# Rounding the stick-breaking heads of a decoder layer in pairs and placing their operands by transfers

## The chip, the cores and the metric

The kernel runs on one core of one Trainium2 chip. The core has TensorE (PE; its weight loads are listed apart as PEld), VectorE (DVE), ScalarE (ACT), GpSimd (POOL) and SyncE (SP), which here issues transfers only. The metric is the device time of one execution in microseconds (us). Inputs and outputs are float32.

## The reference

One layer of a decoder with two groups of attention heads, for 512 tokens of width 2048, and a last RMSNorm:

```python
h = rmsnorm(x, ln_mix)
sb_q, sb_k, sb_v, sw_q, sw_k, sw_v = split(h @ w_in)
# group A, 16 heads of 64: causal stick-breaking
z = (q * 64 ** -0.5) @ k.T
log_one_minus = where(s < t, log_sigmoid(-z), 0)
survive = reverse_cumsum(log_one_minus) - log_one_minus
sb_o = where(s < t, exp(log_sigmoid(z) + survive), 0) @ v
# group B, 16 query heads on 4 key heads: window of 128, ALiBi, sinks, softmax
sw_o = softmax(scores - slope * distance, with a sink) @ v
x = x + concat(rmsnorm(sb_o), rmsnorm(sw_o)) @ w_out
x = x + (silu(h2 @ w_gate) * (h2 @ w_up)) @ w_down      # h2 = rmsnorm(x, ln_ffn)
return rmsnorm(x, ln_final)
```

## The kernel before

**Products.** TensorE multiplies in a rounded float32 form. To keep the accuracy, an operand is split into a high part (a rounded copy) and a low part (the operand minus that copy), and a product is three matmuls: high by high, high by low, low by high. Weights stream from HBM in slabs of 128 x 1024 elements into three buffers `raw`; ScalarE writes the high part `whi` (L215) and VectorE the low part `wlo` (L216), both with two buffers.

**The queue of slabs.** All projections stand in one list, `queue`. Each entry is a slab with its eight products. `step()` emits one product. At the third product of slab i it emits the loads of slabs i+1 and i+2 and the rounding (`split`) of slab i+1. `pull(ns)` emits products worth so many nanoseconds, and `drain(mark)` emits all up to a mark. `defer(n, fn)` calls `fn` after n more products. Loads go through `dma()` (L100), which issues from SP and keeps the order of the program on that queue; the instructions of the other engines may be put in another order by the scheduler that lays out the program, within what their data allow.

**The stick-breaking stage** (about 155 to 433 us). `sb_begin(h)` starts head h. The queries and keys of a pair of heads come out of two PSUM banks into a tile `qk` (L683 and L686), head 2u in rows 0 to 63 and head 2u+1 in rows 64 to 127. A score matmul contracts over 128 rows, so for each head three tiles are made: `q1` has the high part of the queries in both halves, `q2` the low part in both halves, and `ks` the high part of the keys in the rows of the head and the low part in the others. `stack_two` (L692 to L695) and `stack_one` (L701, L702) write them by ScalarE and VectorE, 64 rows at a time. Two matmuls (L846, L847) then give the whole score.

Each head has three jobs, key blocks 3 and 2 together, then 1, then 0. A job passes through the score matmuls, a mask (L852), three ScalarE steps, the split of the log terms (L866, L867, L872), the sums (L904), the exponential and its split (L918, L919, L924) and the product with the values (L934). Jobs are interleaved over three turns of one loop, and in each turn three pulls put products of the queue between the parts. `sb_begin` is called three jobs before the first job of its head. The products in between belong to the later pairs' queries and keys (`add_qk`), then to the window group's keys, and then to its values (`add_swv`).

**The window group's values.** `add_swv` uses `add_tok` with `halves=True`: two blocks of 128 tokens share a PSUM bank, and the last slab runs block by block. `done` evacuates a block by L267 and L268 into `swv`.

**The window stage.** It makes a table of distances `dist` (L977 to L981, first read at L1076), stacks keys and queries of the first key group with the same two helpers, and adds the slabs of query groups 2 and 3 to the queue. Its first score matmuls are at L1061 and L1062.

The window stage's filler continues with the output projection; the feed-forward part, from about 700 us on, is written out in a fixed order and is not touched.

Of the kernel before, what the change touches and what calls it, by code (L numbers as in the profile page):

```python
# [8 lines left out]
F32 = mybir.dt.float32  # L9
F32R = mybir.dt.float32r  # L10
BF16 = mybir.dt.bfloat16
I32 = mybir.dt.int32
AF = mybir.ActivationFunctionType
ALU = mybir.AluOpType
AX = mybir.AxisListType

P = 128
# [4 lines left out]
HD = 64  # L22
# [7 lines left out]
FAR = 1.0e32  # L30
# [7 lines left out]
def tile_hymba(ctx: ExitStack, tc: tile.TileContext, x, ln_mix, w_in, sb_norm, swa_norm,  # L38
# [36 lines left out]
    def pz():  # L75
        return zs[1].tile([P, 512], F32, tag="z", name="z", bufs=4)
# [17 lines left out]
    def tmp(dt=F32, name="t"):  # L94
        return phase[1].tile([P, 512], dt, tag="t", name=name, bufs=phase[2])
# [3 lines left out]
    def dma(out, in_):  # L99
        tc.keep_in_program_order(nc.sync.dma_start(out=out, in_=in_))  # L100

    def f(ap):
        return ap.bitcast(F32)

    mm = nc.tensor.matmul
    V = nc.vector
    A = nc.scalar
    G = nc.gpsimd
# [63 lines left out]
    pos = [0, 0]  # L172
# [26 lines left out]
    def split(i):  # L199
        sl = queue[i]  # L200
        if "hi" in sl:
            return
        load(i)
        if sl["prep"] and i:
            sl["prep"]()
        a, b, raw = sl["a"], sl["b"], sl["raw"]
        hi = wp.tile([P, a, b], F32R, tag="whi", name="whi", bufs=2)
        lo = wp.tile([P, a, b], F32R, tag="wlo", name="wlo", bufs=2)
        if i == 0:
            for j in range(a):  # L210
                h_make(j)
                pA.activation(out=hi[:, j, :], in_=raw[:, j, :], func=AF.Copy)
                pV.tensor_tensor(out=lo[:, j, :], in0=raw[:, j, :], in1=f(hi)[:, j, :], op=ALU.subtract)
        else:
            A.activation(out=hi, in_=raw, func=AF.Copy)  # L215
            V.tensor_tensor(out=lo, in0=raw, in1=f(hi), op=ALU.subtract)  # L216
        sl["hi"], sl["lo"] = hi, lo

    def defer(n, fn):
        due.append([n, fn])  # L220
# [39 lines left out]
    def drain(mark=None):  # L260

        mark = len(queue) if mark is None else mark
        while pos[0] < mark:
            step()
# [54 lines left out]
    def h_make(kt):  # L319
        pb = pz()  # L320
        for t in range(NT):
            pT.transpose(out=pb[:, t * P:(t + 1) * P], in_=xs[kt, t], identity=ident)
            warm({(0, 0): 1, (0, 1): 1, (0, 2): 3, (1, 3): 3}.get((kt, t), 0))
        if kt % 4 == 0:
            h8[0], h8[1] = act8("hhi"), act8("hlo")
        h_hi[kt], h_lo[kt] = h8[0][:, kt % 4, :], h8[1][:, kt % 4, :]
        split_scaled(pb, gcol[:, kt:kt + 1], h_hi[kt], h_lo[kt])
        if kt % 4 == 0:
            h8s.append((h8[0], h8[1]))
        left_sums(kt, pb)  # L330
# [33 lines left out]
    def add_tok(src_fn, nslab, a, b, lhs_fn, get_banks, done, prep_fn=None, halves=False, big=False):  # L364

        bk = {}
        t3 = 3 * 0.4215 * b

        def one(t, j, s):
            def go(hi, lo):  # L370
                k = s * a + j
                lh, ll = lhs_fn(k)
                o = bk["b"][t // 2][:, (t % 2) * b:(t % 2) * b + b] if halves else bk["b"][t][:, :b]
                sl = slice(t * P, (t + 1) * P)
                first = k == 0 and not (halves and t % 2)
                mm(o, lhsT=lh[:, sl], rhs=hi[:, j, :], start=first, stop=False, skip_group_check=halves)  # L376
                mm(o, lhsT=lh[:, sl], rhs=lo[:, j, :], start=False, stop=False, skip_group_check=halves)  # L377
                mm(o, lhsT=ll[:, sl], rhs=hi[:, j, :], start=False, stop=(k == nslab * a - 1),  # L378
                   skip_group_check=halves)
                if k == nslab * a - 1:  # L380
                    done(t, o)
                return t3
            return go

        for s in range(nslab):
            if s == nslab - 1 or (s == 0 and queue):
                mms = [one(t, j, s) for t in range(NT) for j in range(a)]
            else:
                mms = [one(t, j, s) for j in range(a) for t in range(NT)]
            pair = ([] if s % 2 == 0 else pair) if big else None  # L390
            queue.append(dict(srcs=[src_fn(s)], a=a, b=b, mms=mms, big=pair,
                              pre=(lambda: bk.update(b=get_banks())) if s == 0 else None, post=None,
                              prep=(lambda s=s: prep_fn(s)) if prep_fn else None))
# [291 lines left out]
    def k_evac(pb, dst):  # L685
        V.tensor_tensor(out=dst, in0=pb, in1=rs1["b"], op=ALU.mult)  # L686

    def stack_two(src, r0, hi, lo):

        s64 = src[r0:r0 + HD]  # L690
        r1 = HD - r0
        A.activation(out=hi[r0:r0 + HD], in_=s64, func=AF.Copy)  # L692
        V.tensor_copy(out=hi[r1:r1 + HD], in_=s64)
        V.tensor_tensor(out=lo[r0:r0 + HD], in0=s64, in1=f(hi)[r0:r0 + HD], op=ALU.subtract)
        V.tensor_copy(out=lo[r1:r1 + HD], in_=f(lo)[r0:r0 + HD])  # L695

    def stack_one(src, r0, st):

        s64 = src[r0:r0 + HD]
        r1 = HD - r0  # L700
        A.activation(out=st[r0:r0 + HD], in_=s64, func=AF.Copy)  # L701
        V.tensor_tensor(out=st[r1:r1 + HD], in0=s64, in1=f(st)[r0:r0 + HD], op=ALU.subtract)  # L702
# [38 lines left out]
    def sbt(dt, name, n=512, bufs=1):  # L741
        return phase[1].tile([P, n], dt, tag=name, name=name, bufs=bufs)
# [62 lines left out]
    kqp = kqs.enter_context(tc.tile_pool(name="kq2", bufs=1, side="right", reuse_waits="tile"))  # L805
# [2 lines left out]
    sb_mark = len(queue)  # L808
    add_swv()
    swv_end = len(queue)  # L810
    pair = [sbt(F32R, name, 512) for name in ("h32", "l32")]
    for t in pair:
        G.memset(f(t)[:, 0:P], 0.0)
    sqA = kqp.tile([P, 512], F32, name="sqA")

    class Head:
        pass

    heads = {}

    def sb_begin(h):
        drain(marks[h // 2])
        H = Head()
        heads[h] = H
        H.r0 = (h % 2) * HD
        qk = qks[h // 2]
        H.q1, H.q2, H.ks = sbt(F32R, "q1", bufs=2), sbt(F32R, "q2", bufs=2), sbt(F32R, "ks", bufs=2)
        stack_two(qk[:, 0, :], H.r0, H.q1, H.q2)
        stack_one(qk[:, 1, :], H.r0, H.ks)
        H.acc = [None] * 3  # L830
        H.blk = [None] * 3

    def span(i):
        return {2: (P, 512), 1: (0, 384), 0: (0, 512)}[i]

    def sb_qk(h, i):
        H = heads[h]
        B = Head()
        H.blk[i] = B
        a, w = span(i)  # L840
        zb = pz()
        B.zb, B.z = zb, zb[:, a:w]
        for k, c0, o in (((3, 256, 0), (2, 256, 256)) if i == 2 else ((i, i * P, 0),)):
            kb = H.ks[:, k * P:(k + 1) * P]
            out = zb[:, o:o + S - c0]
            mm(out, lhsT=kb, rhs=H.q1[:, c0:S], start=(o == 0), stop=False, skip_group_check=True)  # L846
            mm(out, lhsT=kb, rhs=H.q2[:, c0:S], start=False, stop=True, skip_group_check=True)  # L847
# [106 lines left out]
    for j in range(NJ + 2):  # L954
        if j + 3 < NJ and jobs[j + 3][1] == 2:
# [16 lines left out]


    swp = open_phase("swp", 15)
    dist = swp.tile([P, 256], F32, name="dist", bufs=1)
    disti = tmp(I32, "disti")[:, 0:256]
    G.iota(disti, pattern=[[-1, 256]], base=P, channel_multiplier=1)  # L977
    V.tensor_copy(out=dist, in_=disti)
    G.affine_select(out=dist, in_=dist, pattern=[[-1, 256]], compare_op=ALU.is_ge, fill=FAR,
                    base=P, channel_multiplier=1)  # L980
    G.affine_select(out=dist, in_=dist, pattern=[[1, 256]], compare_op=ALU.is_ge, fill=FAR,  # L981
                    base=-1, channel_multiplier=-1)
    sqB = swp.tile([P, 512], F32, name="sqB", bufs=1)
    oB = [swp.tile([P, 4, 512], F32, tag="oB", name="oB", bufs=2) for _ in range(2)]
    kst = [None, None]
# [2 lines left out]
    def stack_keys(c, e):  # L988
        stack_two(kq2[:, c, :], e * HD, kst[c][:, 2 * e, :], kst[c][:, 2 * e + 1, :])
# [7 lines left out]
    def add_swq(g):  # L997
        def done(c, pb):
            if c == 0:
                qst[g] = v8.tile([P, 4, 512], F32R, tag="v8", name="qst")  # L1000
            qf = tmp(name="qf")
            q_evac(pb, qf)
            for e in range(2):
                stack_one(qf, e * HD, qst[g][:, c * 2 + e, :])

        add_feat(win, [(C_SWQ + g * 256, 256)], (lambda: [po(), po()]) if g == 2 else two_m, done)
        smarks[g] = len(queue)

    kst[0], qst[0], qst[1], kst[1] = (v8.tile([P, 4, 512], F32R, tag="v8", name=n) for n in ("kst", "qst", "qst", "kst"))
    stack_keys(0, 0)  # L1010
    stack_queries(0, 0)
    stack_queries(0, 1)
    for g in (2, 3):
        add_swq(g)


    mixA = [None] * 10
# [835 lines left out]
```

## Time and profile before

| | |
|---|---|
| runs | 2003.01, 2003.05, 2002.39 us; median 2003.01 us |
| profiled execution | 2003.03 us, span 2000.9 us |
| TensorE busy | 1983.5 us (99%) |
| VectorE busy | 1479.4 us (74%) |
| ScalarE busy | 1512.2 us (76%) |
| GpSimd busy | 1115.7 us (56%) |

Rows of waits read "engine line <- engine tile line: us in total, times, longest us". A row of the timeline gives the start and the duration in us, engine, line, operation, output and inputs, shape, and in brackets the idle time before it and what ended it. A row of a tile's view gives minimum, median and maximum in ns and the first and last start. A row of stretches gives the stretch, its length, then the busy time of PE, PEld, DVE, ACT and POOL with the number of instructions, the granted clock, the share of the DMA engines and GB/s. Issues of transfers end with KB each and the median us from issue to landing.

### The profile page before, as it was taken

The numbers are of one execution on the slowest core, as the hardware profiler recorded it, in microseconds if no ns is written. First come the engines' busy times: TensorE is split into PE (matmuls) and PEld (weight loads), VectorE is DVE, ScalarE is ACT, GpSimd is POOL, SyncE is SP. The second block draws the span as 40 slices with busy tenths as digits, with TensorE's granted clock in tenths as the row PEclk, the third lists the DMA queues.
The fourth block names the chain that finished last, engine by engine and source line by source line (L and its number), as shares of the span: only waits on it lengthen the run. The fifth ranks groups of instructions, "written<-read, shape, count | busy, mean of one in ns | idle before, by whom it ended". The sixth has DMA issues, their size and how long they took to land.

```text
span 2000.9 us, 29118 instructions
## 1 busy us (share of the span) xinstructions
PE 1983.5 (99%) x10268; PEld 1697.5 (85%) x10268; DVE 1479.4 (74%) x1972; ACT 1512.2 (76%) x2031; POOL 1115.7 (56%) x599
## 2 busy tenths in 40 slices
PE   9999999999999999999999999999999999999998
PEld 8888888888888888888888888888888888888886
DVE  6677787778974787777777777777777867767767
ACT  6766887868762487777777777777777788788787
POOL 2842454520010076575666657566665778878883
PEclk9999999999999999999999999999999999999999
DMA  6412222222334435445354444535444744433423
GB/s 202 146 53 85 64 65 68 70 71 67 106 115 138 143 121 137 128 110 142 100 138 110 127 126 112 141 101 138 109 129 111 271 150 129 167 126 113 177 80 116
DMA packets 283298, 240.22 MB, mean 120 GB/s; under 512 B 11025, under 2 KB 233297, under 8 KB 280721
## 3 DMA queue, kind: packets, MB, share of 16 engines
q1 hardware_dynamic: 281392, 231.52, 38.9%
q0 software_dynamic: 1376, 5.52, 0.9%
q8 instruction: 81, 1.33, 0.3%
q10 hardware_dynamic: 384, 1.34, 0.2%
q14 instruction: 65, 0.52, 0.1%
HBM read 218.40 MB, written 19.92 MB: 119 GB/s over the span
## 4 chain that ended last, share of the span: by engine, by line
PE 93%; DVE 3%; ACT 3%; issue 1%; DVEq 0%; POOL 0%; ACTq 0%; POOLq 0%
PE o L118 36%; PE m L118 30%; PE m L408 3%; PE m L409 3%; PE m L410 2%; PE m L376 2%; PE m L378 2%; PE m L377 2%; PE z L118 1%; PE o L378 1%; PE o L376 1%; PE o L377 1%; PE z L904 1%; PE o L934 1%; PE z L1112 1%
## 5 line engine op out<-in xcount | busy, mean ns | idle before, releaser
L118 POOL TENSOR_TENSOR t<-raw,t 128x1024 f32<-128x1024 f32 x111 | 282.3, 2543 | 281.1 <-ACT hp L118 262.8
L118 DVE TENSOR_TENSOR wlo<-t,hp 128x1024 fp32r<-128x1024 f32 x247 | 301.0, 1219 | 183.2 <-PE o L118 113.6
L118 ACT ACTIVATE whi<-t 128x1024 fp32r<-128x1024 f32 x247 | 261.9, 1060 | 126.3 <-PE o L118 76.3
L118 POOL TENSOR_TENSOR t<-raw,raw 128x1024 f32<-128x1024 f32 x114 | 294.7, 2588 | 23.5 <-issue 12.1
L118 PE MATMUL o<-hca,whi 128*128 128x512 f32 x880 | 307.5, 391 | 0.0
L118 DVE TENSOR_TENSOR wlo<-raw,hp 128x1024 fp32r<-128x1024 f32 x187 | 228.1, 1220 | 91.7 <-issue 52.1
L118 ACT ACTIVATE whi<-raw 128x1024 fp32r<-128x1024 f32 (+1 forms) x189 | 199.8, 1057 | 105.4 <-PE m L118 75.2
L118 ACT ACTIVATE hp<-t 128x1024 fp32r<-128x1024 f32 x247 | 249.1, 1009 | 2.2 <-POOL t L118 2.1
L118 PE MATMUL o<-hca,wlo 128*128 128x256 f32 x880 | 244.0, 280 | 0.0
L118 ACT ACTIVATE hp<-raw 128x1024 fp32r<-128x1024 f32 x191 | 192.9, 1010 | 4.4 <-DMA raw<-in_w_down_dram 3.2
L118 PEld LDWEIGHTS o<-hca,whi 128*128 128x128 f32 x880 | 164.2, 187 | 35.8
L118 PE MATMUL m<-hca,whi 128*128 128x512 f32 x528 | 186.3, 392 | 1.1 <-DVE hca L118 1.1
L118 PEld LDWEIGHTS o<-hca,wlo 128*128 128x128 f32 x880 | 165.6, 189 | 0.4
L215 ACT ACTIVATE whi<-raw 128x1024 fp32r<-128x1024 f32 x87 | 91.7, 1054 | 79.8 <-PE o L378 39.2
L216 DVE TENSOR_TENSOR wlo<-raw,whi 128x1024 fp32r<-128x1024 f32 x87 | 108.7, 1249 | 56.0 <-ACT whi L215 53.7
L118 PE MATMUL m<-whi,dca 128*128 128x512 f32 x592 | 146.9, 389 | 0.0
L118 PE MATMUL o<-whi,dca 128*128 128x512 f32 x592 | 146.9, 389 | 0.0
L118 PE MATMUL m<-hca,wlo 128*128 128x256 f32 x528 | 146.3, 280 | 0.0
L118 PEld LDWEIGHTS m<-whi,dca 128*128 128x128 f32 x592 | 111.1, 188 | 23.1
L118 PEld LDWEIGHTS o<-whi,dca 128*128 128x128 f32 x592 | 111.1, 188 | 23.0
L408 PE MATMUL m<-hhi,whi 128*128 128x512 f32 x320 | 125.9, 393 | 0.7 <-DVE qk L683 0.7
L118 PE MATMUL m<-hcs,whi 128*128 128x512 f32 x352 | 125.9, 392 | 0.0
(371 smaller groups left out, 5225.8 us busy)
## 6 DMA issues: line engine op xcount, KB each, us to landing
raw<-in_w_gate_up_dram SPq DMA_DIRECT2D x348, 256.0 KB, 5.2
raw<-in_w_down_dram SPq DMA_DIRECT2D x68, 512.0 KB, 4.9
raw<-in_w_in_dram SPq DMA_DIRECT2D x35, 512.0 KB, 3.7
raw<-in_w_in_dram SPq DMA_DIRECT2D x66, 256.0 KB, 3.3
raw<-in_w_out_dram SPq DMA_DIRECT2D x32, 512.0 KB, 3.7
aT<-w SPq DMA_DIRECT2D x44, 256.0 KB, 3.4
xd<-aT SPq DMA_DIRECT2D x10, 1024.0 KB, 7.5
rx<-in_w_down_dram SPq DMA_DIRECT2D x20, 512.0 KB, 6.2
```

Of the source, the lines that this page charges most:

```text
L118: return lambda *a, **k: tc.keep_in_program_order(fn(*a, **k))
L215: A.activation(out=hi, in_=raw, func=AF.Copy)
L216: V.tensor_tensor(out=lo, in0=raw, in1=f(hi), op=ALU.subtract)
L376: mm(o, lhsT=lh[:, sl], rhs=hi[:, j, :], start=first, stop=False, skip_group_check=halves)
L377: mm(o, lhsT=lh[:, sl], rhs=lo[:, j, :], start=False, stop=False, skip_group_check=halves)
L378: mm(o, lhsT=ll[:, sl], rhs=hi[:, j, :], start=False, stop=(k == nslab * a - 1), skip_group_check=halves)
L408: mm(o, lhsT=wh, rhs=xh, start=(k == 0), stop=False)
L409: mm(o, lhsT=wh, rhs=xl, start=False, stop=False)
L410: mm(o, lhsT=wl, rhs=xh, start=False, stop=(k == KT - 1))
L904: mm(zb[:, o:o + r.shape[1]], lhsT=lhsT, rhs=r, start=False, stop=last, skip_group_check=True)
L934: mm(H.ob[:, c0:S], lhsT=vb, rhs=r[:, o:o + S - c0], start=(k == 3 and r is B.h), stop=(k == 0 and r is B.l), skip_group_check=True)
L1112: nc.tensor.transpose(out=pb[:, hh * P:(hh + 1) * P], in_=B.s[hh // 2][:, hh % 2, j * P:(j + 1) * P], identity=ident)
```

## The change

Four things are changed.

1. `sb_begin` rounds a pair at once: for an even head, `hi_lo` writes the high parts of the pair's queries and of its keys into a new tile `qkh` (ScalarE, 128 rows each) and leaves the low parts in `qk` itself (VectorE, 128 rows each). A function `place`, called six products later or at the head's first score matmuls at the latest, fills `ks`, `q1` and `q2` by six transfers of 64 rows on SP.
2. In `add_tok` with halves, both blocks of a bank are evacuated after the second one.
3. The table `dist` is made before the stick-breaking loop, in the pool that holds `sqA`, whose tile lends its first half to the integers.
4. At the start of the window stage the slabs of the queries are queued first, and the next slab is rounded before the keys and queries are stacked. That stacking stays with the engines.

```diff
                 if k == nslab * a - 1:
-                    done(t, o)
+                    if not halves:
+                        done(t, o)
+                    elif t % 2:
+                        done(t - 1, bk["b"][t // 2][:, 0:b])
+                        done(t, o)
...
+    def hi_lo(src, hi):
+        A.activation(out=hi, in_=src, func=AF.Copy)
+        V.tensor_tensor(out=src.bitcast(F32R), in0=src, in1=f(hi), op=ALU.subtract)
...
+    dist = kqp.tile([P, 256], F32, name="dist")
+    sqA = kqp.tile([P, 512], F32, name="sqA")
+    disti = sqA[:, 0:256].bitcast(I32)
+    G.iota(disti, pattern=[[-1, 256]], base=P, channel_multiplier=1)
+    V.tensor_copy(out=dist, in_=disti)
+    G.affine_select(out=dist, in_=dist, pattern=[[-1, 256]], compare_op=ALU.is_ge, fill=FAR,
+                    base=P, channel_multiplier=1)
+    G.affine_select(out=dist, in_=dist, pattern=[[1, 256]], compare_op=ALU.is_ge, fill=FAR,
+                    base=-1, channel_multiplier=-1)
...
-        H.q1, H.q2, H.ks = sbt(F32R, "q1", bufs=2), sbt(F32R, "q2", bufs=2), sbt(F32R, "ks", bufs=2)
-        stack_two(qk[:, 0, :], H.r0, H.q1, H.q2)
-        stack_one(qk[:, 1, :], H.r0, H.ks)
+        if h % 2 == 0:
+            qkh[0] = sbt(F32R, "qkh", 1024).rearrange("p (two t) -> p two t", two=2)
+            for c in range(2):
+                hi_lo(qk[:, c, :], qkh[0][:, c, :])
+
+        def place():
+            H.place = None
+            H.q1, H.q2, H.ks = sbt(F32R, "q1", bufs=2), sbt(F32R, "q2", bufs=2), sbt(F32R, "ks", bufs=2)
+            rows = slice(H.r0, H.r0 + HD)
+            for r in (0, HD):
+                dma(out=f(H.ks)[r:r + HD], in_=(f(qkh[0]) if r == H.r0 else qk)[rows, 1, :])
+            for r in (0, HD):
+                dma(out=f(H.q1)[r:r + HD], in_=f(qkh[0])[rows, 0, :])
+            for r in (0, HD):
+                dma(out=f(H.q2)[r:r + HD], in_=qk[rows, 0, :])
+
+        H.place = place
+        defer(6, lambda: H.place and H.place())
...
+        if H.place:
+            H.place()
         zb = pz()
...
     kst[0], qst[0], qst[1], kst[1] = (v8.tile([P, 4, 512], F32R, tag="v8", name=n) for n in ("kst", "qst", "qst", "kst"))
+    for g in (2, 3):
+        add_swq(g)
+    split(pos[0] + 1)
     stack_keys(0, 0)
     stack_queries(0, 0)
     stack_queries(0, 1)
-    for g in (2, 3):
-        add_swq(g)
```

More of the change, by code (lines that the diff above doesn't have):

```diff
@@ L813, in tile_hymba @@
         G.memset(f(t)[:, 0:P], 0.0)
-    sqA = kqp.tile([P, 512], F32, name="sqA")
     class Head:
@@ L819, in tile_hymba @@
     heads = {}
+    qkh = [None]
     def sb_begin(h):
@@ L974, in tile_hymba @@
     swp = open_phase("swp", 15)
[L975 to L982, printed above, removed]
     sqB = swp.tile([P, 512], F32, name="sqB", bufs=1)
```

## The prediction

> **What bounds the kernel now.** I read the page's first section, then the engine's busy time in stretches, then who waits for whom on TensorE alone.
>
> ```profile
> span 2000.9 us, 29118 instructions
> PE 1983.5 (99%) x10268; PEld 1697.5 (85%) x10268; DVE 1479.4 (74%) x1972; ACT 1512.2 (76%) x2031; POOL 1115.7 (56%) x599
> 140.00:160.00 20.00, 20.00 (x91) 16.29 (x91) 15.48 (x23) 11.27 (x19) 0.00 (x0) 1.00 0.30 88
> 240.00:420.00 180.00, 176.63 (x886) 150.34 (x885) 141.81 (x220) 145.99 (x261) 89.62 (x116) 1.00 0.22 65
> 1980.00:2001.00 21.00, 11.52 (x50) 8.94 (x48) 14.06 (x35) 12.79 (x33) 5.55 (x5) 0.90 0.55 200
> PE o L934 <- DVE l L924: 2.6, 4, 1.2
> PE m L376 <- DVE swv L268: 1.6, 1, 1.6
> PE m L408 <- DVE qk L683: 0.7, 2, 0.4
> ```
>
> TensorE (first busy column of a stretch) is idle for 17.4 us of the span, and 9.5 of these are the tail (21.00 minus 11.52), which the change does not touch. No matmul is added or removed. So the change can only win idle time of TensorE in the stick-breaking stage (about 155 to 433 us) and at its end, or add some. There the last three rows are all there is: seven waits, 4.9 us.
>
> The idle column understates a stop, because a matmul's modelled end overlaps the next one's start:
>
> ```profile
> 356.00 0.28 PE L934 MATMUL o<-h,vst 128*128 128x256 f32 x1
> 356.70 0.39 PE L934 MATMUL o<-l,vst 128*128 128x256 f32 x1 [0.43 <-DVE l L924]
> 356.92 0.28 PE L934 MATMUL o<-h,vst 128*128 128x256 f32 x1
> 357.04 0.28 PE L934 MATMUL o<-l,vst 128*128 128x256 f32 x1
> ```
>
> Unhindered, such matmuls start 0.12 us apart (the last two); here 0.70 passed, so 0.58 was lost where the row says 0.43. I add 0.16 for each wait: L934 2.6 + 4 × 0.16 = 3.25, L408 0.7 + 2 × 0.16 = 1.05, L376 1.6 + 0.16 = 1.75. The **ceiling of the gain is 6.05 us**, 0.3% of the run.
>
> **The parts that free engines.** A pair of heads is now rounded by four full-height instructions instead of twelve half-height ones.
>
> ```profile
> L692 ACT ACTIVATE q<-qk x16: 618/631/632, 156.2 to 382.5; 64x512 fp32r<-64x512 f32 x16
> L693 DVE CAST q<-qk x16: 420/423/855, 156.2 to 383.6; 64x512 fp32r<-64x512 f32 x16
> L694 DVE TENSOR_TENSOR q<-qk,q x16: 683/688/1211, 157.1 to 384.4; 64x512 fp32r<-64x512 f32 x16
> 274.28 0.61 ACT L867 ACTIVATE h<-e 128x512 fp32r<-128x512 f32 x1
> 275.82 0.68 DVE L872 TENSOR_TENSOR l<-e,h 128x512 fp32r<-128x512 f32 x1
> ```
>
> Lines 701, 702 and 695 cost as 692, 694 and 693 do, the same operations on the same shape. VectorE spent 0.42 + 0.69 + 0.42 + 0.69 = 2.22 us a head, 35.5 in all; full height costs the same per instruction (0.68), so two of them a pair are 8 × 1.36 = 10.9. ScalarE goes from 16 × 1.26 = 20.2 to 8 × 1.22 = 9.8. VectorE thus gets 24.6 us and ScalarE 10.4 back in a stage where they are busy 79% and 81%. That alone wins nothing; it wins only what the stops above owe to this stacking. What stood ahead of them on VectorE, with the stops that followed:
>
> ```profile
> 354.51 0.95 DVE L702 TENSOR_TENSOR ks<-qk,ks 64x512 fp32r<-64x512 f32 x1
> 289.03 0.95 DVE L702 TENSOR_TENSOR ks<-qk,ks 64x512 fp32r<-64x512 f32 x1
> 292.79 0.39 PE L934 MATMUL o<-l,vst 128*128 128x256 f32 x1 [0.22 <-DVE l L924]
> 273.37 1.23 DVE L216 TENSOR_TENSOR wlo<-raw,whi 128x1024 fp32r<-128x1024 f32 x1 [0.63 <-ACT whi L215]
> 275.96 0.38 PE L934 MATMUL o<-l,vst 128*128 128x256 f32 x1 [0.80 <-DVE l L924]
> ```
>
> Two of the four stops at L934 (356.70 and 292.79) come behind stacking: 0.43 + 0.22 + 2 × 0.16 = 0.97 us, which I count as won. The other two, 3.25 − 0.97 = 2.28 us (the first at 275.96 above), come behind a slab's low part (L216), before which VectorE stood idle: that stop belongs to the order of the queue, not to its load. The two at L408 (1.05) have no stacking in front either. Of these 3.33 us a lighter load can win all or nothing; since idle time preceded the slab's part, I take a third, 1.1.
>
> **The swv drain.** With two token blocks in one bank, block 1's matmuls waited for block 0's evacuation: 1.75 us. Now both evacuations follow block 1, and blocks 2 and 3 go to the other bank, so nothing waits: 1.75 us won. TensorE then comes 1.75 us sooner to what follows, which has these covers:
>
> ```profile
> 432.15 0.42 DVE L695 CAST kst<-kst 64x512 fp32r<-64x512 f32 x1
> 436.58 0.40 POOL L981 TENSOR_SCALAR_AFFINE_SELECT dist<-dist 128x256 f32<-128x256 f32 x1
> 436.80 0.28 PE L1061 MATMUL z<-kst,qst 128*128 128x256 f32 x1
> 437.49 1.06 ACT L215 ACTIVATE whi<-raw 128x1024 fp32r<-128x1024 f32 x1
> 438.07 0.86 DVE L1076 SCALAR_TENSOR_TENSOR s<-dist,z 128x128 f32<-128x128 f32 x4
> 439.74 0.40 PE L408 MATMUL o<-hhi,whi 128*128 128x512 f32 x1
> 440.21 0.39 PE L408 MATMUL o<-hhi,whi 128*128 128x512 f32 x1
> 440.79 0.39 PE L410 MATMUL o<-hhi,wlo 128*128 128x512 f32 x1
> ```
>
> The table (`dist`) was ready at 436.98 and first read at 438.07; 1.75 earlier it would have been late by 0.66. Made in the stage's opening it costs GpSimd nothing (idle from 140 to 160 in the stretch above) and VectorE one copy. The first weight slab of the next queries, rounded by 438.55 and first used at 439.74, would likewise be late by 0.56; rounded before the key stacking it is early, and pushes the stacking back by its low part, 1.23. The stacking ended 4.23 us ahead of its first reader (436.80 minus 432.57): 4.23 − 1.75 − 1.23 leaves 1.2. I cost both at nothing; uncovered, they would give back 0.7 and 0.6.
>
> **The transfers.** Each head gets six, of 64 rows × 2 KB = 128 KB, 96 in all on SP, in program order among the weight loads. No transfer from SBUF to SBUF stands in this trace; the nearest rows:
>
> ```profile
> L100 SPq DMA_DIRECT2D raw<-in_w_in_dram x60: 367/368/1260, 149.8 to 412.0; - x60
> DMA to landing us min/median/max: 2.7/3.4/5.1
> xd<-aT SPq DMA_DIRECT2D x10, 1024.0 KB, 7.5
> 158.97 0.69 DVE L686 TENSOR_TENSOR qk<-m,rbc 128x512 f32<-128x512 f32 x1
> 162.75 0.28 PE L846 MATMUL z<-q,ks 128*128 128x256 f32 x1
> 345.36 0.69 DVE L686 TENSOR_TENSOR qk<-m,rbc 128x512 f32<-128x512 f32 x1
> 352.15 0.28 PE L846 MATMUL z<-q,ks 128*128 128x256 f32 x1
> ```
>
> For an even head they cannot start before its keys are evacuated (L686, end E), copied (0.6) and subtracted (0.7). The second needs E + 1.4; four more issues of 0.37 put the sixth at E + 2.9, and 3.4 us of landing (the weight loads, mostly 256 KB) at **E + 6.3**. Between E and the first score matmul stood 3.1 us for head 0 and 6.1 for head 12 (the rows above); the eight even heads in order had 3.1, 9.8, 8.4, 7.2, 8.1, 6.8, 6.1 and 6.9. At E + 6.3 head 0 is late by 3.2 and head 12 by 0.2. The shortest landing, 2.7, leaves head 0 late by 2.5; below that a smaller transfer may fall, and at nothing late the cost is nil. The upper bound: if the six land like one transfer of 1 MB, 7.5 us from the first issue, E + 8.2 and 11 us late in sum. I take the weight loads, nearest in size. Whether lateness stops TensorE depends on the instruction order. Matmuls can be ordered past one that is not ready: at 440.21 a second product with the slab's high part (L408) ran before the first with its low part (L410 at 440.79), against the order of the code. A late head 0 may be passed by filler products the same way, so I take half of 3.4: **1.7 us lost**. Odd heads read a pair that was rounded a head earlier; their transfers are covered.
>
> The Trainium skill (SBUF — State Buffer, "Door 1: the DMA port swizzle (why [64,N] ≈ [32,N])") speaks against this form: a 64-partition transfer reaches half of the ports, about 196 GB/s, and two on different halves serialize. By it six of 128 KB would take an estimated 4.0 us plus its fixed 2 us, so land near E + 6.7 instead of E + 6.3. No row here shows such a transfer.
>
> Weight loads queued behind these transfers on SP are held until E + 1.4 at most, and then by 2.2 us of issuing. Their cover:
>
> ```profile
> 357.81 0.37 SPq L100 DMA_DIRECT2D raw<-in_w_in_dram  x1
> 377.20 1.04 ACT L215 ACTIVATE whi<-raw 128x1024 fp32r<-128x1024 f32 x1
> ```
>
> With three raw buffers the load issued at 357.81 is first read two slabs past the next, at 377.20: 19.4 us, less 3.4 of landing, leaves 16. A load written after a head's transfers is read at least eight products, some 8 us, later than they are written, so I cost the hold at nothing; without that cover it would be the same few microseconds per pair.
>
> **Sum.** The profiled execution took 2003.03 us (span 2000.9 and 2.1 around it; the median of the runs is 2003.01). 2003.03 − 1.75 − 0.97 − 1.1 + 1.7 = **2000.9 us**.
>
> **The rivals.** *All stops go* and filler passes the late first head: 2003.03 − 6.05 = 1997.0. For it: 24.6 us off VectorE in that stage. Against: idle time before L216.
> *The transfers come late at every pair*, the case on the slower side: the place is the first score matmul of an even head, and it decides from E + 6.3 on. If the keys' low part has a slab's L216 (1.2) ahead of it, the six land at E + 7.5: late by 4.4, 0.3, 0.7, 1.4 and 0.6 at heads 0, 6, 10, 12 and 14, 7.4 together, with no filler passing: 2003.03 − 1.75 − 0.97 + 7.4 = 2007.7. For it: the margins, and in-order SP. Against: the order evidence at 440. The port rule of the Trainium skill named above belongs to this rival.
> *The change does not relieve*: the stops are dealt anew behind L216 at the same number, and head 0 is late by half: 2003.03 − 1.75 + 1.7 = 2003.0.
>
> **How the numbers follow.** Forecast 0.45 (own range 1999 to 2002.6), all stops go 0.23, late transfers 0.20, no relief 0.12. About 0.2%, 4.0 us, is what a measurement of this kernel can tell from no change. Faster by more: the second case and a fifth of the first, 0.32. Slower by more: most of the late case, 0.16. The rest, 0.52, is within. The range runs from the ceiling to the late case, 1996.5 to 2008.
>
> **What would show it.** Right: no wait for L268 on TensorE near 434; VectorE's stacking lines gone from before L924; at most two waits of L934 and one of a score matmul on a transfer, at head 0. Wrong: waits of L846 or L847 for a transfer at several even heads (the transfers' landing time then says which bound held), waits of the slab rounding for a late raw load, or a new wait near 436 for the table, the keys or the slab.

## The result and the profile after

The changed kernel takes 1997.99 us (median of 12 runs, 1997.02 to 1999.47) against 2002.95 us (median of 12, 2002.16 to 2003.73): a ratio of 0.9976, 95% interval 0.9968 to 0.9984, or 5.0 us less. Here and below, the medians are of the fast runs; three executions that took far longer, one of the kernel before and two of the run with the whole load put back, are left out. The profiled execution took 1997.55 us with a span of 1995.8. Around the span lie 1.75 us now and 2.1 before, so 0.35 us of the gain are outside the span. These 0.35 us are there in every run of the kernels with the pair rounding, and in the run that moves casts to GpSimd; the run with only the other three parts has 2.1 us again. Why, no run shows. In the changed file, the slab products of lines 408 to 410 are lines 412 to 414, the score matmuls 880 and 881, the mask 886, the split of the weights 958 and the value matmuls 968.

The page's first rows, the stretches of the stage and of the tail (columns as before), and TensorE's waits from 140 to 440 us, of the changed kernel:

```profile
span 1995.8 us, 29234 instructions
PE 1982.6 (99%) x10268; PEld 1696.9 (85%) x10268; DVE 1444.9 (72%) x1924; ACT 1501.2 (75%) x2015; POOL 1109.0 (56%) x599
240.00:420.00 180.00, 179.31 (x916) 154.17 (x916) 123.99 (x195) 142.22 (x257) 84.55 (x116) 1.00 0.43 112
1975.00:1996.00 21.00, 11.39 (x49) 8.83 (x47) 13.95 (x35) 12.67 (x33) 5.45 (x5) 0.83 0.55 200
PE z L881 <- DMA q<-qk: 0.7, 1, 0.7
```

TensorE's idle time in the span went from 17.4 to 13.2 us, and the tail has about as much of it as before (9.6 us, before 9.5). In the stage, TensorE gained 2.7 us of work in the stretch from 240 to 420. All seven stops of before are gone and one new one is there, a score matmul that waits for a transfer. VectorE lost 17.8 us in that stretch (141.81 to 123.99).

The tile views and the issues from 150 to 420 us show the new parts:

```profile
L693 ACT ACTIVATE qkh<-qk x16: 614/632/635, 155.8 to 375.1; 128x512 fp32r<-128x512 f32 x16
L694 DVE TENSOR_TENSOR qk<-qk,qkh x16: 686/693/1227, 156.5 to 376.3; 128x512 fp32r<-128x512 f32 x16
L100 SPq DMA_DIRECT2D q<-qkh x32: 587/594/1952, 161.1 to 383.4; - x32
L100 SPq DMA_DIRECT2D ks<-qk x16: 462/467/904, 160.6 to 381.6; - x16
q<-qkh SPq DMA_DIRECT2D x32, 128.0 KB, 3.4
q<-qk SPq DMA_DIRECT2D x32, 128.0 KB, 2.4
ks<-qkh SPq DMA_DIRECT2D x16, 128.0 KB, 3.5
ks<-qk SPq DMA_DIRECT2D x16, 128.0 KB, 3.0
```

A full-height instruction costs what a half-height one did (medians of 0.63 us on ScalarE and 0.69 on VectorE, both as before). A transfer of 128 KB lands 2.4 to 3.5 us after its issue by the medians of the four groups; single ones took 2.2 to 7.4 us. Issuing one takes 0.47 to 0.60 us. A weight load took 0.37 before; in the changed kernel it takes 0.51 as well.

**Where a stop went.** The stop of 0.80 us at 275.96 shows it best, because in both kernels the instructions of the three engines from 263 us up to it are the same, in the same order. The timeline of before, from the score matmul that opens this job to the split of the weights, and then of after, to the value matmul:

```profile
266.94 0.39 PE L847 MATMUL z<-q,ks 128*128 128x512 f32 x1
269.62 0.28 DVE L852 TENSOR_TENSOR z<-z,maskf 128x128 f32<-128x128 f32 x1
275.35 0.56 DVE L924 TENSOR_TENSOR l<-e,h 128x384 fp32r<-128x384 f32 x1
```

```profile
266.90 0.39 PE L881 MATMUL z<-q,ks 128*128 128x512 f32 x1
268.42 0.29 DVE L886 TENSOR_TENSOR z<-z,maskf 128x128 f32<-128x128 f32 x1
272.18 1.23 DVE L216 TENSOR_TENSOR wlo<-raw,whi 128x1024 fp32r<-128x1024 f32 x1 [0.63 <-ACT whi L215]
274.15 0.56 DVE L958 TENSOR_TENSOR l<-e,h 128x384 fp32r<-128x384 f32 x1
274.96 0.28 PE L968 MATMUL o<-l,vst 128*128 128x256 f32 x1
```

The score matmul starts at the same time. From the mask to the split passed 5.73 us in both, with the slab's low part in the same place and the same 0.63 us of idle before it. But the mask came 2.68 us after the score matmul before, and 1.52 us after it now. So the lateness did not arise at the slab; it was there already at the mask. Some 15 us ahead of that mask one sees it grow. Before, and then after:

```profile
253.94 0.56 DVE L866 SCALAR_TENSOR_TENSOR e<-z,e 128x384 f32<-128x384 f32 x1 [0.64 <-issue]
253.88 0.63 ACT L692 ACTIVATE q<-qk 64x512 fp32r<-64x512 f32 x1
254.41 0.61 ACT L701 ACTIVATE ks<-qk 64x512 fp32r<-64x512 f32 x1
254.73 1.20 DVE L694 TENSOR_TENSOR q<-qk,q 64x512 fp32r<-64x512 f32 x1
255.05 0.53 ACT L867 ACTIVATE h<-e 128x384 fp32r<-128x384 f32 x1
257.32 0.95 DVE L702 TENSOR_TENSOR ks<-qk,ks 64x512 fp32r<-64x512 f32 x1
```

```profile
253.14 0.56 DVE L900 SCALAR_TENSOR_TENSOR e<-z,e 128x384 f32<-128x384 f32 x1 [1.23 <-ACT e L895]
253.79 0.53 ACT L901 ACTIVATE h<-e 128x384 fp32r<-128x384 f32 x1 [0.74 <-DVE e L900]
```

The chain's step on VectorE (L866, now L900) already ran 0.80 us later before. Then two copies of an odd head stood ahead of its next step on ScalarE, which ran at 255.05; now an odd head has nothing there, and the step runs at 253.79, 1.26 us sooner. On VectorE the stacking of the same head (L694, L695, L702) followed until 258.27, and the next L866 came at 258.31, where its counterpart L900 now comes at 256.49, 1.82 us sooner. From 263 us on, the distance between the two kernels stays at 1.2 us up to the mask and on to the stop. So the mask's 1.2 us arose in this stretch, with the odd head's stacking in both queues; the rows do not part ScalarE's share from VectorE's.

### The profile page after: what moved, and what is told of

The parts are those of the page before. It is cut to its first block, busy times and chain, and to the rows that moved or that the text cites. A ratio compares the mean times of both kernels' runs of the same rounds, so it can differ in the third digit from the quotient of the medians.

```text
span 1995.8 us, 29234 instructions
## 1 busy us (share of the span) xinstructions
PE 1982.6 (99%) x10268; PEld 1696.9 (85%) x10268; DVE 1444.9 (72%) x1924; ACT 1501.2 (75%) x2015; POOL 1109.0 (56%) x599
## 4 chain that ended last, share of the span: by engine, by line
PE 96%; ACT 2%; DVE 1%; issue 0%; DMA 0%; SPq 0%; DVEq 0%; POOL 0%; ACTq 0%; POOLq 0%
PE o L118 36%; PE m L118 30%; PE m L412 3%; PE m L413 3%; PE m L414 3%; PE m L376 2%; PE m L378 2%; PE m L377 2%; PE z L938 2%; PE z L118 1%; PE o L376 1%; PE o L378 1%; PE o L377 1%; PE o L968 1%; PE z L1139 1%; PE z L881 0%
## 5 line engine op out<-in xcount | busy, mean ns | idle before, releaser
L412 PE MATMUL m<-hhi,whi 128*128 128x512 f32 x320 | 125.8, 393 | 0.0
```

Of the source, the lines that this page charges most:

```text
L412: mm(o, lhsT=wh, rhs=xh, start=(k == 0), stop=False)
```

## The experiments

The idle TensorE time below is each run's own row of waits. A stop costs some 0.16 us more than its row says, as the prediction showed. All ratios are to the kernel before, of runs on the same chip (its medians there are 2002.9 us each time). Their intervals reach about 1.8 us to either side: the gain of the whole change is clear, but differences of a microsecond or two between the runs rest on the rows of their profiles and not on the medians alone.

### The two halves of the change

*Only the pair rounding and the transfers*, with parts 2, 3 and 4 as before:

```diff
-                    if not halves:
-                        done(t, o)
-                    elif t % 2:
-                        done(t - 1, bk["b"][t // 2][:, 0:b])
-                        done(t, o)
+                    done(t, o)
...
+    dist = swp.tile([P, 256], F32, name="dist", bufs=1)
...
-    for g in (2, 3):
-        add_swq(g)
-    split(pos[0] + 1)
     stack_keys(0, 0)
     stack_queries(0, 0)
     stack_queries(0, 1)
+    for g in (2, 3):
+        add_swq(g)
```

> Only the pair rounding and the placing by transfers; evacuation of the value banks, table and slab order as before. Theory (the stops in the stick-breaking stage are what the rounding in pairs removes): 3.25 + 1.05 us won at L934 and L408, 0.84 lost at one score matmul, the 1.75 us wait for swv is still there: about 1999.5 us. Rival (most of the gain is in the other three parts): about 2002.

Measured 2001.02 us, ratio 0.9991 (0.9982 to 1.0). It gained 1.9 us, not the 3.5 expected. The stops in the stage are gone as the theory said. The rest is in two views, the waits of TensorE and the stretches around the value drain, and in the timeline behind the stop:

```profile
PE m L376 <- DVE swv L268: 2.2, 1, 2.2
PE z L869 <- DMA q<-qk: 0.8, 1, 0.8
432.00:434.00 2.00, 1.92 (x12) 1.92 (x13) 0.32 (x2) 0.00 (x0) 1.46 (x4) 0.76 0.00 0
434.00:436.00 2.00, 2.00 (x12) 2.00 (x11) 1.18 (x4) 1.69 (x3) 0.04 (x1) 0.50 0.00 0
436.00:438.00 2.00, 2.00 (x17) 2.00 (x17) 1.71 (x5) 0.16 (x1) 0.00 (x0) 0.89 0.00 0
434.29 0.41 PE L378 MATMUL m<-whi,hlo 128*128 128x256 f32 x1
434.50 0.41 PE L1083 MATMUL z<-kst,qst 128*128 128x256 f32 x1
```

The wait for `swv` grew from 1.6 to 2.2 us, and behind it the granted clock (the column after the engines) fell to 0.50. Matmuls of 256 columns then started 0.21 us apart instead of 0.12. Some sixteen of them ran so between 433.0 and 436.4, about 1.5 us lost on top of the stop. In the kernel before, the same stop of 1.6 us left the clock at full rate:

```profile
434.00:436.00 2.00, 0.98 (x8) 0.98 (x9) 0.74 (x2) 0.45 (x1) 1.60 (x2) 1.00 0.00 0
```

*Only the other three parts*, with the stacking by engines as before (the edit is the reverse: parts 2, 3 and 4 applied, `sb_begin` unchanged):

```diff
         H.q1, H.q2, H.ks = sbt(F32R, "q1", bufs=2), sbt(F32R, "q2", bufs=2), sbt(F32R, "ks", bufs=2)
         stack_two(qk[:, 0, :], H.r0, H.q1, H.q2)
         stack_one(qk[:, 1, :], H.r0, H.ks)
```

> Stacking by engines as before, and only the three other parts: both evacuations after the second block, table early, slab rounded first. Theory: 1.75 us won, about 2001.2 us, the seven stops of L934 and L408 as before. Rival (TensorE, coming sooner, waits for something else there): no gain, about 2003.

Measured 2001.28 us, ratio 0.9992 (0.9983 to 1.0001): 1.6 us less, as expected. Its waits are those of before without the row for `swv` (six stops; the expectation says seven):

```profile
PE o L946 <- DVE l L936: 2.6, 4, 1.2
PE m L412 <- DVE qk L687: 0.7, 2, 0.4
```

The halves alone give 1.9 and 1.6 us, 3.5 together; the whole change gives 5.0. The 1.5 us between are as much as the first half pays for the low clock, which the second half removes; medians with these intervals could not show a difference of that size by themselves.

*The whole change without the joint evacuation:*

```diff
-                    if not halves:
-                        done(t, o)
-                    elif t % 2:
-                        done(t - 1, bk["b"][t // 2][:, 0:b])
-                        done(t, o)
+                    done(t, o)
```

> The changed kernel with the evacuation of the value banks as before (block by block). Theory: the wait for swv on TensorE comes back. With only the transfers it was 2.2 us and the granted clock was 0.50 in the 2 us behind it, where half-rate matmuls cost an estimated 1.5 us more; so about 1997.9 + 2.3 + 1.5 = 2001.7 us, or 2000.2 where the clock holds. Rival (the early slab and table already cover the stop): 1998.

Measured 2001.56 us, ratio 0.9992 (0.9983 to 1.0001): the joint evacuation is worth 3.6 us here. In the profiled execution (2001.32 us) the stop is back with 2.1 us and the clock falls again:

```profile
PE m L376 <- DVE swv L268: 2.1, 1, 2.1
434.00:436.00 2.00, 2.00 (x11) 2.00 (x11) 1.11 (x4) 1.62 (x3) 0.00 (x0) 0.50 0.00 0
```

Four of the eleven executions took only 1999.48 to 2000.42 us, near the 2000.2 that were expected where the clock holds. So the clock may not fall in each execution; only one has a trace.

*The whole change without the early table and the early slab:*

```diff
-    dist = kqp.tile([P, 256], F32, name="dist")
...
+    dist = swp.tile([P, 256], F32, name="dist", bufs=1)
...
-    split(pos[0] + 1)
```

(the slabs of the queries are queued behind the stacking again)

> The changed kernel with the table made at the start of the window stage and the slab rounded after the stacking, as before. By the prediction these two hide at most 0.7 and 0.6 us: 1998 to 1999.3 us, with waits near 435 for the slab rounding if any. Rival (they carry the gain of the drain): 1999.7 us or more.

Measured 1998.79 us, ratio 0.998 (0.9972 to 0.9989). The 0.8 us against the whole change are too little for such a comparison to tell, but the profile has a stop of that size where none was, and it is the slab's:

```profile
PE o L412 <- ACT whi L215: 1.0, 1, 1.0
```

No wait for the table shows. What moving the table alone gives was not run.

### Whose load makes the stops

*Work put back on VectorE,* whole and in part (two instead of five instructions):

```diff
+        dum = sbt(F32R, "dum", 192)[H.r0:H.r0 + HD]
+        src, top = (x[H.r0:H.r0 + HD, 0, 0:192] for x in (qk, f(qkh[0])))
+        for k in range(5):
+            if k % 2:
+                V.tensor_copy(out=dum, in_=src)
+            else:
+                V.tensor_tensor(out=dum, in0=src, in1=top, op=ALU.subtract)
```

> The changed kernel, with idle work on VectorE at the start of every head: three subtractions and two copies of 64 x 192 into a scratch tile, an estimated 1.6 us a head from the 128 and 256 column rows, as much as the rounding in pairs took off. Theory A (a lighter VectorE removes the stops): stops before the second value matmul or the slab products return, two to four of them, 2000 to 2001.5 us. Theory B (the order of the queues was dealt anew, the load does not matter): no stops, about 1998.

> The changed kernel with one subtraction and one copy of 64 x 192 into a scratch tile on VectorE per head, an estimated 0.6 us of the 1.6 us that brought four stops back. Theory A (the stops follow VectorE's load): one or two stops before the second value matmul, 1998.5 to 2000.5 us. Theory B (any added instruction deals the order anew): as many stops as with the whole load, 2002.

The whole load: 2001.95 us, ratio 0.9996 (0.9987 to 1.0006), 4.0 us above the changed kernel and a little above the stretch of theory A. The part: 1999.63 us, ratio 0.9985 (0.9976 to 0.9994). TensorE's waits of the one and of the other:

```profile
PE o L976 <- DVE l L966: 3.7, 4, 1.2
```

```profile
PE o L976 <- DVE l L966: 1.2, 1, 1.2
PE z L889 <- DMA q<-qk: 0.7, 2, 0.4
```

Four stops come back, then one. Theory A holds against theory B: an added instruction alone does not bring all the stops, more load brings more of them. They are all at the value matmuls; those at the slab products (L408, now L412) do not come back.

*Work put back on ScalarE:*

```diff
+        dum = sbt(F32R, "dum", 192)[H.r0:H.r0 + HD]
+        src = qk[H.r0:H.r0 + HD, 0, 0:192]
+        for k in range(2):
+            A.activation(out=dum, in_=src, func=AF.Copy)
```

> The changed kernel with two copies of 64 x 192 into a scratch tile on ScalarE per head, an estimated 0.6 us, what the rounding in pairs took off ScalarE. Theory (VectorE, which does the last step before the second value matmul, decides): no stops, 1998 us. Rival (ScalarE's chain ahead of it decides, since VectorE stood idle before the slab part): stops return, 2000 us or more.

Measured 2000.98 us, ratio 0.9991 (0.9982 to 1.0). The theory fell and the rival held: ScalarE's load brings stops too.

```profile
PE z L886 <- DMA q<-qk: 1.7, 2, 0.9
PE o L973 <- DVE l L963: 0.7, 2, 0.4
```

Two are stops before the second value matmul. The larger part is at the transfers of heads 6 and 12, which start later (for head 6 at 251.46 us instead of 249.19) and land later. The chain of a job passes ScalarE and VectorE in turn, and here work put in front of ScalarE alone delayed it.

*Load taken off the kernel before:* the two casts of a head's queries moved to GpSimd, with no pair and no transfer.

```diff
-    def stack_two(src, r0, hi, lo):
+    def stack_two(src, r0, hi, lo, eng=V):
...
-        V.tensor_copy(out=hi[r1:r1 + HD], in_=s64)
+        eng.tensor_copy(out=hi[r1:r1 + HD], in_=s64)
...
-        V.tensor_copy(out=lo[r1:r1 + HD], in_=f(lo)[r0:r0 + HD])
+        eng.tensor_copy(out=lo[r1:r1 + HD], in_=f(lo)[r0:r0 + HD])
...
-        stack_two(qk[:, 0, :], H.r0, H.q1, H.q2)
+        stack_two(qk[:, 0, :], H.r0, H.q1, H.q2, G)
```

> The kernel before, with the two casts of every stick-breaking head's queries moved from VectorE to GpSimd: VectorE loses 0.84 us a head without any transfer or pair. Theory A (load): one to three of the six stops in the stage go, 2000 to 2002 us. Theory B: the six stops stay or others come, 2002.5 us or more. A subtraction then waits for nothing of GpSimd, but the first score matmuls do.

Measured 2000.88 us, ratio 0.999 (0.9981 to 0.9999): 2.0 us less with a lighter VectorE and a busier GpSimd, 0.35 of them outside the span. Two of the four stops before the second value matmul went, and the longest shrank:

```profile
PE o L934 <- DVE l L924: 1.3, 2, 0.8
PE m L408 <- DVE qk L683: 0.7, 2, 0.5
```

Both that went are the two with stacking right ahead; the two at the slab fell from 2.28 to 1.6 us, and those of L408 stayed. VectorE's busy time in the stage (155 to 433 us) against the stops at the value matmuls and at L408, ordered by load: 218.2 us in the kernel before, 4.9 − 1.6 = 3.3 us of idle; 210.1 with the whole load, 3.7; 204.9 with the casts moved, 2.0; 196.9 with the part, 1.2; 187.5 in the changed kernel, none. More load, more stops, if not strictly in step. VectorE's load is not all of it: the run with the copies on ScalarE has 0.7 us at 186.5, and the next run below 0.5 at 188.3, with nothing added to any engine.

### The transfers

*The queries' four transfers ahead of the keys' two:*

```diff
-            for r in (0, HD):
-                dma(out=f(H.ks)[r:r + HD], in_=(f(qkh[0]) if r == H.r0 else qk)[rows, 1, :])
             for r in (0, HD):
                 dma(out=f(H.q1)[r:r + HD], in_=f(qkh[0])[rows, 0, :])
             for r in (0, HD):
                 dma(out=f(H.q2)[r:r + HD], in_=qk[rows, 0, :])
+            for r in (0, HD):
+                dma(out=f(H.ks)[r:r + HD], in_=(f(qkh[0]) if r == H.r0 else qk)[rows, 1, :])
```

> The changed kernel with the four transfers of the queries ahead of the two of the keys. The queries are rounded some 3 us before the keys, so their transfers go out while SP now waits for the keys. Theory (the one stop left, 0.84 us at head 12, is the last transfer landing late): the stop goes, about 1997.2 us. Rival (holding SP longer makes weight loads late): new waits of the slab rounding for a load, 1998.5 us or more.

Measured 1997.76 us, ratio 0.9975 (0.9966 to 0.9985). The stop at the score matmul is gone, and another of 0.5 us stands before a value matmul:

```profile
PE o L968 <- DVE l L958: 0.5, 1, 0.5
```

The time is that of the changed kernel, as far as can be told; whether it is 0.2 us better stays open.

*No deferral,* so that the transfers are written right before a head's first score matmuls:

```diff
-        defer(6, lambda: H.place and H.place())
```

> The changed kernel without the deferral of six products: the transfers of a head are written right before its first score matmuls. Theory (what counts is when SP reaches them and what the scheduler puts in between; filler passes the late score matmuls): the chain of each head is later, few stops of TensorE, 1998 to 2001 us. Rival (order kept): each of 16 heads waits for six issues of 0.6 us and a landing of 3 us, 5 us and more each, 2080 us.

Measured 1997.96 us, ratio 0.9976 (0.9967 to 0.9985): no difference. Head 0's six transfers went out at the same distance from its rounding as with the deferral, so SP seems to run ahead of the place where the code writes a transfer.

*Every transfer issued twice:*

```diff
-            for r in (0, HD):
+            for r in (0, HD) * 2:
```

(in each of the three loops; the second copy writes what the first wrote, and waits for it)

> The changed kernel with every one of the 96 transfers issued twice in a row. Theory (transfers are late only at head 12, by 0.8 us, and the others have about 1 us of margin): six more issues of 0.6 us land the last operand some 3.7 us later; stops of score matmuls at most even heads, 2 to 3 us each where the order holds, 2005 to 2018 us; near 1999 if filler passes them. Rival (transfers have cover to spare): no change, 1998.

Measured 2013.7 us, ratio 1.0053 (1.004 to 1.0065): 15.7 us above the changed kernel, inside the expected stretch, but not by its mechanism. No score matmul waits; the scheduler put filler ahead of them. The filler then ran out behind head 0, and the clock fell there as well. The waits and two stretches:

```profile
PE z L938 <- POOL ah L919: 3.0, 1, 3.0
PE z L938 <- POOL al L922: 1.5, 1, 1.5
175.00:179.00 4.00, 0.98 (x6) 0.47 (x4) 1.80 (x6) 3.65 (x9) 0.78 (x3) 1.00 0.46 103
181.00:183.00 2.00, 1.80 (x6) 1.71 (x7) 1.23 (x1) 0.17 (x1) 2.00 (x3) 0.51 0.91 199
```

The expectation that passing filler would keep the time near 1999 thus failed. These stops and the low clock make up some 6 of the 15.7 us; by the starts of the matmuls most of the rest lies in some fifty small delays of 0.1 to 0.5 us each, most of them at L938, the sums of the score chain. It was not taken apart further.

## Why the prediction was right, and where its sizes were off

**Bound and ceiling.** Right: TensorE's stops in the stage and at the drain were what there was to win in the span, 6.05 us. All seven went and one of 0.84 came, which leaves 5.2; the profiled span fell by 5.1. What came true was nearly the rival in which all stops go: 2003.03 − 6.05 + 0.84 and the 0.35 outside the span make 1997.5, and the profiled execution took 1997.55. The prediction took the time around the span as fixed.

**The forecast.** The way and the place were right, the size was not: 2.1 us less were forecast (2000.9), 5.0 came. Two terms erred, both to the same side: 1.1 us where 3.33 were won, and 1.7 us where 0.84 were lost. The 1997.99 us lie within the whole range of 1996.5 to 2008, but below the 1999 to 2002.6 of the forecast case itself. Of the chances for what a measurement can tell, the largest, 0.52, stood on a change too small to tell; 0.32 stood on a gain of more than 4.0 us, which came.

**The swv drain.** Right in place and size: 1.75 us were put on it, the three parts alone gave 1.6. Inside the whole change the joint evacuation is worth 3.6, because without it the stop there is longer and, in the profiled execution, costs clock; the prediction had not seen that.

**The covers.** Mechanism right for the slab (0.56 us late was foreseen, a stop of 1.0 came without the cover); the table's was never seen to count, and moving the table back alone was not run.

**The stops behind a slab.** Here the forecast was too small. The mis-sized term is "a third, 1.1" of 3.33 us: all 3.33 were won. The reason given for a third, that VectorE stood idle before the slab's low part and so load was not the cause, was wrong. At the stop at 275.96 the idle time was a wait for ScalarE's chain, and that chain had been late since a stacking some 20 us ahead of the stop; the mask of the job shows it (2.68 us behind its score matmul, now 1.52). At the other, at 390.17 and the longest of all with 1.20 us, VectorE had hardly been idle before the slab's low part:

```profile
387.83 1.23 DVE L216 TENSOR_TENSOR wlo<-raw,whi 128x1024 fp32r<-128x1024 f32 x1 [0.17 <-ACT whi L215]
```

Its mask came 3.99 us behind the score matmul (384.05 after 380.06), now 2.42, and two stacking instructions (L702 at 380.00, L693 at 383.60) stood on VectorE in between. The two stops at L408, 1.05 of the 3.33 us, went too, but by what stays open: they stayed when the casts left VectorE, and did not come back when load was put back on VectorE or ScalarE. The two stops directly behind stacking (0.97) were counted rightly.

**What the engines got back.** VectorE's busy time in the stage fell by 30.7 us where 24.6 were worked out from medians; the half-height instructions had run longer than their median there (43.4 us in all, where 35.5 were worked out). ScalarE's fell by 8.3 where 10.4 were expected.

**The transfers.** 1.7 us of lateness were put on them, most of it at head 0; 0.84 came, at head 12. Head 0's score matmuls were passed by filler, wholly and not by half. Head 12 was the tightest of the rest, and there the late rival's mechanism did occur. The timeline of the changed kernel from the evacuation of its keys on:

```profile
341.85 0.68 DVE L690 TENSOR_TENSOR qk<-m,rbc 128x512 f32<-128x512 f32 x1
343.53 1.29 DVE L216 TENSOR_TENSOR wlo<-raw,whi 128x1024 fp32r<-128x1024 f32 x1 [0.34 <-ACT whi L215]
344.74 1.22 DVE L694 TENSOR_TENSOR qk<-qk,qkh 128x512 fp32r<-128x512 f32 x1
347.78 1.24 SPq L100 DMA_DIRECT2D q<-qk  x2
350.99 0.36 PE L881 MATMUL z<-q,ks 128*128 128x256 f32 x1 [0.69 <-DMA q<-qk]
```

A slab's low part stood ahead of the keys', and issuing took 0.6 us a transfer instead of 0.37, so the last one landed near E + 8.4 instead of E + 6.3 (E is 342.53). It did not come to this at every pair because the cover had grown: from head 4 on the evacuations came sooner against the score matmuls, and the seven later even heads had 7.5 to 9.0 us instead of 6.1 to 9.8. That the lighter engines brought this is likely but not shown. Little cover is left: doubling the transfers cost 15.7 us, if by other stops than this rival's.

By the Trainium skill (SBUF — State Buffer, "Door 1: the DMA port swizzle (why [64,N] ≈ [32,N])") the six would end at an estimated E + 6.7 for their half of the ports. The median landings of 2.4 to 3.5 us do not contradict it. But at head 12 the last transfer was issued only at about E + 5.9, behind the rounding's place in VectorE's queue and five other issues, and landed some 2.5 us later; no run separated the ports.

**SP.** Weight loads behind held transfers cost nothing, as said: in the changed kernel no stop of TensorE goes back to a late raw load.

## What to carry to other kernels

An engine that is idle just before the late instruction is not thereby cleared: follow its chain back to the first step that started late against TensorE, which may lie several jobs earlier, and ask what stood in the queue there. Load in front of a chain that passes two engines counts on both, even where each is only 80% busy, as here. Parts of a change that each look worth a microsecond can be worth more together, when one lengthens a stop beyond the point where the clock drops (here between 1.6 and 2.1 us) and another removes it.

## What was not expected of the hardware

TensorE's granted clock reacted to a single short stop. A stop of 1.6 us, in the kernel before, left it at 1.00. Stops of 2.1 and 2.2 us were followed by a stretch at 0.50: with the transfers alone, TensorE's last free start before the stop was at 429.6, it resumed at 432.1, the matmuls became slower at 432.9 and were at full rate again from 436.5. The stop thus cost 2.3 + 1.5 us. The Trainium skill (TensorE: Matmul & The Clock Gate, "Part 1: The HAM clock gate (the "warmup" mystery)") has the half rate come after an idle window of about 3.4 us; here it came after 2.1 us of idling, and the measurement decides. The lower rate held for about 3.5 us, which is about that window's length.
